# A mixer-and-FFN layer on one core: staging of the first projection, order of units, and where softmax is normalized

## The chip, the cores and the metric

The kernel runs on one core of a Trainium2 chip. The metric is the device time of one execution in microseconds (us); lower is better. The engines are TensorE (PE: matmuls, and PEld for its weight loads), VectorE (DVE), ScalarE (ACT), GpSimd (POOL) and SyncE (SP). SP and POOL only issue transfers here; the sixteen DMA engines carry them. Each engine takes its instructions in the order in which the program lists them.

## What is computed

One layer of a streaming encoder over 1088 tokens: 1024 of a new stream (the prompt) and 64 of a running one (the sample), of width 1024.

```python
h    = rmsnorm(x, g_mix)
cb, cc, ch, q, k, v, ga, gb = split(h @ w_in)      # 512 x6, 1024 x2 columns
ya   = (cb * causal_conv3(cc * ch)) @ w_conv_out
s    = q @ k.T / 8 + rel_bias[clip(i - j)]          # band: own chunk of 64 and 8 before; 8 heads of 64
o    = softmax(s) @ v                               # sample: keys and values of the caches too
yb   = o @ w_attn_out
x    = x + (sigmoid(ga) * ya + sigmoid(gb) * yb) @ w_out
x    = x + (silu(n @ w1) * (n @ w3)) @ w2           # n = rmsnorm(x, g_ffn)
y    = rmsnorm(x, g_final)
```

Besides y, the kernel stores the rolled caches: the newest 512 key and value rows of the prompt and of the sample (for the sample 448 old rows and 64 new ones), and two rows of the convolution's input for each.

## The kernel before

Every product is done in fp32 by parts: `split` (L117, L118) makes a high part by a cast on ACT and a low part by a subtraction on DVE, and three matmuls (high x high, high x low, low x high; L292 to L294 in `product`, or L456 to L458) add up one product. A transfer from or to DRAM is issued by SP unless said otherwise.

The stages, in order of time:

1. *First projection* (0 to 97 us). The nine token tiles go through in the order 8, 0, 1, 4, 2, 5, 3, 6, 7 (`ORDER`). `load_x` fetches a tile into one of three slots of 1024 columns in the scratch tile `scr`; `normed` squares it on ACT into the slot SQ (L382), makes the factor, and scales the tile on DVE with `gm` (L384), which L367 writes once; `turned1` transposes it on TensorE (L398), and casts and sums of it follow. `v_tile` multiplies it with the weights of v, and `put_v` splits the result into a single slot VST and stores it to `v_d`. The values of the last 512 prompt tokens and of the sample are also copied into SQ (L462) and stored to the outputs by POOL. Meanwhile POOL copies bias tables 0 and 1 from DRAM to DRAM (tile 3 of the order) and 448 rows of each cache to the outputs (tile 5).
2. *Twelve units* (to 365 us). Each is one pair of 128-column blocks of q, k, cc, ch, cb or gb, by Strassen's scheme (L234); ACT's L222 and L525 and DVE's adds bring its sums out of PSUM. In this stage `cache_tile` splits the old rows of the caches for k_d and v_d, and x_d and u_d (convolution's result) are written.
3. *Gates and attention* (to 614 us). Twelve gate blocks `g` (each four pieces of 24 matmuls, 128x272) are computed from weights whose load and split run ahead (`prep`, tiles rawp, whp, wlp), and stored to ga_d and gb_d. After a piece, `between` advances attention by PER steps, as long as it has any. A step does the scores of one tile of 128 queries of a head (L836, L837), its `softmax` (maximum L794, exponential with row sum L804, reciprocal L805, scaling L806), the transposes of the tile two steps back (L866, split into pt), and the values of a pair three steps back (L878, L891) with `combine` (L812 to L814), which writes o_d. At the fourth tile (t = 3) of a head, `head_load` issues the loads of k, q, v and bias of the next head, and the copy of a later bias table is asked for; the memsets L784 and L785 then write parts of the bias. Before the last LAST gates all remaining attention steps are drained.
4. *Merge* (645 to 744 us). Where the last LAST gates begin, u is loaded and o in four parts: `ol` (one buffer) is loaded, then split into `ob`. Then for eight column blocks ya = u @ w_conv_out, yb = ob @ w_attn_out, with sigmoid of ga and gb loaded again, give `mg`.
5. *Output projection, FFN up, FFN down* (744 to 1559 us), which the change does not touch.

The instructions of an engine are put in their order when the program is built, by a scheduler that looks at data and buffers; the lines give the dependences, not the order in full.

Of the kernel before, what the change touches and what calls it, by code (L numbers as in the profile page):

```python
# [8 lines left out]
F32 = mybir.dt.float32  # L9
# [27 lines left out]
PER = 2.25  # L37
LAST = 2
# [26 lines left out]
def encoder_kernel(ctx: ExitStack, tc: tile.TileContext, ins, outs):  # L65
# [19 lines left out]
    nc.gpsimd.dma_start(cols[:, :20], ins["cols"])  # L85
# [13 lines left out]
    o_d = dr.tile([ATT, T], F32, name="o_d")  # L99

# [7 lines left out]
    tables = {}  # L108

    def bias_table(h):  # L110

        tables[h] = dr.tile([P * 384], F32, tag="bias_d", name=f"bias_d{h}", bufs=2)
        nc.gpsimd.dma_start(tables[h].rearrange("(p n) -> p n", n=384), bias_rows(h, 384, 384))
# [147 lines left out]

    def prep(upto):
        while prep.n < min(upto, len(plan)):
            ld, kt, at = plan[prep.n]
            if "raw" not in ld:
                raw = rpool.tile([P, kt, ld["w"]], F32, tag="raw", name=f"rawp{prep.n}")
                nc.sync.dma_start(raw, ld["src"].rearrange("(k p) n -> p k n", p=P))
                ld["raw"] = raw
            w = []
            for k in range(0, kt, 4):  # L270
                hi, lo = (ws.tile([P, 4, P], F32R, tag=t, name=f"{t}p{prep.n}_{k}") for t in ("wh", "wl"))
                split(hi, lo, ld["raw"][:, k : k + 4, at : at + P])
                w.append((hi, lo))
            plan[prep.n] = w
            prep.n += 1
# [40 lines left out]
    X, GM, SUMS, KEPT, VST, SQ, FEW = (0, 1024, 2048), 3072, 4096, (5120, 6144), 7168, 8192, 9216  # L316
# [12 lines left out]
    def put_v(st, src, n, row):  # L329
        st = st.bitcast(F32R).rearrange("p (h l d) -> p h l d", h=NH, l=2)  # L330
        s = src.rearrange("p (h d) -> p h d", h=NH)
        split(st[:n, :, 0, :], st[:n, :, 1, :], s[:n])
        nc.sync.dma_start(
            v_d[:, row : row + n, :].rearrange("h t e -> t h e"),
            st[:n].rearrange("p h l d -> p h (l d)").bitcast(F32),
        )
# [3 lines left out]
    def load_x(i):  # L340
        t0, n = TT[i]
        a = X[len(xts) % 3]
        xts[i] = scr[:, a : a + D]
        nc.sync.dma_start(xts[i][:n], x_rows(i))
# [15 lines left out]
    load_x(ORDER[2])  # L360
# [87 lines left out]
    def v_tile(i):  # L448
# [10 lines left out]
        put_v(scr[:, VST : VST + D], pv, n, t0 if t0 < TP else TP + CACHE)  # L459
# [10 lines left out]
    for nm, u in (  # L470
        ("q", 0), ("q", 1), ("k", 0), ("k", 1), ("gb", 0), ("cc", 0), ("ch", 0), ("cb", 0), ("gb", 1), ("cc", 1),
        ("ch", 1), ("cb", 1),
    ):
        base = {"q": C_Q, "k": C_K, "cc": C_CC, "ch": C_CH, "cb": C_CB, "gb": C_GB}[nm]
        units.append((nm, u, w_in[:, base + 2 * u * P : base + 2 * (u + 1) * P]))
# [10 lines left out]
    for n, i in enumerate(ORDER):  # L486
        if n + 1 < len(ORDER):
            turned1(ORDER[n + 1])
        if n + 3 < len(ORDER):
            load_x(ORDER[n + 3])  # L490
        if n + 2 < len(ORDER):
            normed(ORDER[n + 2])
        if n == 3:
            bias_table(0)
            bias_table(1)
        if n == 4:
            u0 = unit_of(0)
        if n == 5:
            u1 = unit_of(1)

            for nm in ("k", "v"):
                nc.gpsimd.dma_start(
                    outs[f"cache_{nm}_sample"][: CACHE - TS], ins[f"cache_{nm}"].rearrange("t h d -> t (h d)")[TS:]
                )
# [163 lines left out]
    def cache_tile(i):  # L668
        ct = cts[i]
        put_v(slot(CC, 2 * ATT), ct[:, ATT:], P, TP + i * P)  # L670
# [13 lines left out]
    class PlainNext:  # L684
        def prep(self, step):
            if step == 2:
                prep(1)
            elif step == 5:
                prep(2)
# [16 lines left out]
    for n in range(len(units)):  # L706
        if n == 0:
            r, si = r0, 2
        else:
# [3 lines left out]
            else:  # L713
                new = [(PlainNext(), {})]
            if n == 1:
                ahead += new
                r, si = r1, 2
            else:
                r, si = run1(n, unit, new), 0
# [41 lines left out]
    heads = {}  # L761

    def head_load(h):
# [3 lines left out]
        for l in range(2):  # L767
# [14 lines left out]
            b[:, 384:], tables[h][127 : 127 + P * 383].rearrange("(p n) -> p n", n=383)[:, :256]  # L782
# [5 lines left out]
    def softmax(s, ps, bias, n, nm):  # L788
# [3 lines left out]
        sm = at_pool.tile([P, 1], F32, tag="sm", name=f"sm{nm}", bufs=3)[:rows]  # L792
        rc = at_pool.tile([P, 1], F32, tag="rc", name=f"rc{nm}", bufs=3)[:rows]
# [11 lines left out]
        vec.reciprocal(rc, sm)  # L805
        vec.tensor_scalar_mul(s, s, rc)  # L806
# [16 lines left out]
    def scores(h, t):  # L823
# [10 lines left out]
        for i in range(parts):  # L834
# [3 lines left out]
        b0 = 640 - n if t < 8 else 0  # L838
        softmax(
            s[:r, :n], ps[:r, :, :w] if parts == 2 else ps[:r, 0, :w], bias[:r, b0 : b0 + n], n, f"{h}_{t}"  # L840
        )
        return s
# [54 lines left out]
    def attention():  # L897
        order = [(h, t) for h in range(NH) for t in range(9)]
        done = []
        for i in range(len(order) + 3):  # L900
            if i < len(order):
                h, t = order[i]
                if t == 3 and h + 1 < NH:
                    head_load(h + 1)
                    if h + 3 < NH:
                        bias_table(h + 3)
# [21 lines left out]
    bias_table(2)  # L928
    for i in range(2):
        gate_w[i] = next_w()  # L930
        gate(i, (0, 1))
    for i in range(2):
        for c in (2, 3):
            gate(i, (c,))
            if i:
                between()
    for i in range(2, len(GATES)):
        gate_w[i] = next_w()
        if i == len(GATES) - LAST:
# [6 lines left out]
            mp = pg_stack.enter_context(tc.tile_pool(name="mgp", bufs=5, reuse_waits="tile"))  # L946
            for k in range(4):
                nc.sync.dma_start(u.t[:, :, k].bitcast(F32), u_d[k])
                t = mp.tile([P, T], F32, tag="ol", name=f"ol{k}", bufs=1)
                nc.sync.dma_start(t, o_d[k * P : (k + 1) * P])  # L950
                split(ob.t[:, 0, k], ob.t[:, 1, k], t)
# [578 lines left out]
```

## Time and profile before

| | |
|---|---|
| runs | 1568.69 us median of 3 (1564.74 to 1569.67) |
| profiled execution | 1561.12 us, its span 1559.3 us |
| PE busy in the span | 1481.3 us (95%) |
| DVE, ACT, POOL busy | 1008.3, 681.7, 70.5 us |
| granted clock of TensorE, mean | 0.988 |
| largest transfers by bytes | q1 (issued by SP) 203.74 MB, q0 (by POOL) 53.10 MB |

How to read the rows: a row of the timeline holds start, duration, engine, line, operation, output<-input, shapes, and in brackets the idle time of the engine just before with what ended it. In the table of waits there stand total, count and longest. Group rows hold count, busy total, mean ns, then idle time before. A window row holds the busy time of each engine with counts, the granted clock, the share of the DMA engines and GB/s. Transfers have KB each and the us from issue to landing.

### The profile page before, as it was taken

What the parts mean: (1) busy time and instruction counts of PE and PEld (TensorE: products, weight loads), DVE (VectorE), ACT (ScalarE), POOL (GpSimd) and SP (SyncE); (2) the same over time, 40 slices, a digit from 0 to 9 for tenths busy, and PEclk for the clock granted to TensorE, in tenths of its full rate; (3) what the DMA queues carried; (4) which work ended last, traced back from release to release, by engine and by line L of the source; (5) the groups of instructions that cost most, each with busy time, mean ns of one, the idle gap of its engine ahead of it and who ended that gap; (6) DMA issues with size and microseconds to landing.
All of it is one profiled execution on the core that took longest, in us unless ns stands there. A gap on an engine that the chain in (4) does not pass through costs nothing.

```text
span 1559.3 us, 26380 instructions
## 1 busy us (share of the span) xinstructions
PE 1481.3 (95%) x10178; PEld 1387.8 (89%) x10178; DVE 1008.3 (65%) x1989; ACT 681.7 (44%) x1382; POOL 70.5 (5%) x133
## 2 busy tenths in 40 slices
PE   5699999997999999999998999999999999899998
PEld 4589999996989889999787999999999999688886
DVE  4684556552678776566179766666666767846677
ACT  4564433331656665554056444444444444513123
POOL 1100000000000000000000000011011110000000
PEclk9899999998999999999999999999999999999999
DMA  8558654338755543853442333444444347776675
GB/s 265 167 152 218 174 155 66 126 55 242 204 159 159 154 133 110 268 165 111 140 153 95 102 124 129 144 153 144 147 153 144 134 152 261 275 233 233 218 262 204
DMA packets 178269, 260.62 MB, mean 167 GB/s; under 512 B 21328, under 2 KB 118240, under 8 KB 177984
## 3 DMA queue, kind: packets, MB, share of 16 engines
q1 hardware_dynamic: 162400, 203.74, 43.4%
q0 software_dynamic: 14592, 53.10, 9.2%
q10 hardware_dynamic: 1152, 2.10, 0.4%
q8 instruction: 80, 1.31, 0.3%
q14 instruction: 45, 0.37, 0.1%
HBM read 170.41 MB, written 91.89 MB: 168 GB/s over the span
## 4 chain that ended last, share of the span: by engine, by line
issue 73%; PE 17%; POOL 3%; DMA 3%; DVE 2%; ACT 1%; SPq 0%; POOLq 0%; ACTq 0%
PE A L1447 7%; PE D L1447 3%; POOL h_d L1168 2%; PE B L1447 2%; PE Ab L234 1%; DMA w2r<-in_w_ff 1%; PE Aa L234 1%; PE ys L1305 1%; DMA wv<-in_w_in 1%; PE Db L234 1%; PE Da L234 1%; DMA h_d<-hq 0%; PE Bb L234 0%; POOL x_d L1057 0%; POOL x_d L1070 0%
## 5 line engine op out<-in xcount | busy, mean ns | idle before, releaser
L1447 PE MATMUL A<-ring,ht 128*128 128x512 f32 x528 | 125.0, 390 | 4.2 <-ACT acc L1457 2.5
L1447 PEld LDWEIGHTS A<-ring,ht 128*128 128x128 f32 x528 | 98.7, 188 | 26.3 <-ACT acc L1457 3.8
L292 PE MATMUL g<-xn,whp 128*128 128x272 f32 x384 | 113.5, 296 | 1.1 <-ACT scr L525 1.0
L294 PE MATMUL g<-xn,wlp 128*128 128x272 f32 x384 | 112.4, 293 | 0.0
L293 PE MATMUL g<-xn,whp 128*128 128x272 f32 x384 | 112.3, 293 | 0.0
L117 ACT CAST ring<-w2r 128x512 fp32r<-128x512 f32 (+1 forms) x78 | 43.4, 588 | 105.1 <-PE A L1447 51.2
L117 ACT CAST hq<-sa 128x512 fp32r<-128x512 f32 x77 | 47.7, 619 | 85.1 <-DVE sa L1180 56.0
L292 PEld LDWEIGHTS g<-xn,whp 128*128 128x128 f32 x384 | 73.0, 190 | 2.0 <-ACT scr L525 1.2
L118 DVE TENSOR_TENSOR hq<-sa,hq 128x512 fp32r<-128x512 f32 x77 | 53.1, 689 | 33.0 <-ACT hq L117 32.9
L293 PEld LDWEIGHTS g<-xn,whp 128*128 128x128 f32 x384 | 73.1, 190 | 0.7
L294 PEld LDWEIGHTS g<-xn,wlp 128*128 128x128 f32 x384 | 72.9, 190 | 0.1
L118 DVE TENSOR_TENSOR wla<-rawa,wha 128x512 fp32r<-128x512 f32 x56 | 38.4, 687 | 42.3 <-ACT wha L117 42.3
L1447 PE MATMUL D<-ring,ht 128*128 128x512 f32 x264 | 62.9, 390 | 2.0 <-ACT acc L1457 2.0
L234 PE MATMUL Aa<-tt,wha 128*128 128x272 f32 x352 | 60.3, 293 | 3.5 <-ACT tt L117 3.5
L1447 PEld LDWEIGHTS D<-ring,ht 128*128 128x128 f32 x264 | 49.5, 188 | 12.6 <-ACT acc L1457 2.4
L234 PE MATMUL Ab<-tt,whb 128*128 128x272 f32 x352 | 58.9, 288 | 1.6 <-ACT whb L117 1.6
L1168 POOL DMA_DIRECT2D h_d<-hq x77 | 40.9, 532 | 421.2 <-DVE hq L118 244.0
L804 ACT ACTIVATE p<-p,mx 128x640 f32<-128x640 f32 (+5 forms) x72 | 50.9, 707 | 20.2 <-DVE mx L794 19.2
L234 PE MATMUL Ab<-mg,whb 128*128 128x272 f32 x352 | 58.4, 288 | 0.0
L234 PE MATMUL Aa<-mg,wha 128*128 128x272 f32 x352 | 58.3, 288 | 0.0
L117 ACT CAST wha<-rawa 128x512 fp32r<-128x512 f32 x56 | 34.8, 622 | 53.6 <-PE Ab L234 36.6
L118 DVE TENSOR_TENSOR ring<-w2r,ring 128x512 fp32r<-128x512 f32 (+1 forms) x78 | 48.9, 646 | 14.3 <-ACT ring L117 14.1
(510 smaller groups left out, 4346.0 us busy)
## 6 DMA issues: line engine op xcount, KB each, us to landing
h_d<-hq POOLq DMA_DIRECT2D x77, 512.0 KB, 3.5
ht<-h_d SPq DMA_DIRECT2D x154, 256.0 KB, 3.5
rawa<-in_w_ff SPq DMA_DIRECT2D x11, 1024.0 KB, 5.6
rawb<-in_w_ff SPq DMA_DIRECT2D x11, 1024.0 KB, 5.3
w2r<-in_w_ff SPq DMA_DIRECT2D x11, 1024.0 KB, 5.9
qd<-q_d SPq DMA_DIRECT2D x32, 272.0 KB, 4.6
v_d<-scr SPq DMA_DIRECT2D x12, 512.0 KB, 3.4
rawp<-in_w_in SPq DMA_DIRECT2D x6, 1024.0 KB, 12.0
```

The lines of the kernel that those rows point to most:

```text
L117: act.copy(hi, src)
L118: vec.tensor_tensor(lo, src, hi.bitcast(F32), op=ALU.subtract)
L234: mm(t[:, j, :HN], w[:, k, :], x[p][:, l, k, j * HN : (j + 1) * HN], start=p in (1, 2, 7) and k == 0 and n == 0, stop=k == 3 and n == 2, s ...
L292: mm(out, a, p, start=k == 0, stop=False)
L293: mm(out, a, q, start=False, stop=False)
L294: mm(out, b, p, start=False, stop=k == kt - 1)
L804: act.activation(s, s, AF.Exp, bias=mx, scale=-1.0, accum_out=sm)
L1168: nc.gpsimd.dma_start(h_d[p, c - 1], hq.rearrange("p i l t -> p (i l t)").bitcast(F32))
L1305: mm(ys[:, d, a : a + n], hs[:, r], w, start=first and i == at[d][0], stop=final and i == at[d][-1])
L1447: mm(t, ht[k][:, j, x], w[:, l], start=p in (1, 2, 7) and k == 0 and n == 0, stop=k == len(ks) - 1 and n == 2, skip_group_check=p in (6, 5 ...
```

## The change

It does the following, all in one file:

- x is staged in two slots, not three, and the load of a tile is asked for one tile later; v is staged in two slots, not one, and the stores to v_d go by POOL.
- The 448 old rows of both caches are stored by POOL from the tiles loaded in stage 2, not copied from DRAM to DRAM in stage 1. The bias tables of all heads are written at once in the sixth unit, by SP, through a slot of `scr`.
- The two gb units move to the end of the twelve; the first gate weight is loaded from the start of the last unit, and three weights are split during it instead of two.
- Four gates do their first two pieces ahead of attention, not two; PER goes from 2.25 to 2.1 and LAST from 2 to 1.
- `softmax` no longer scales its tile. The row sums of a head's nine tiles are kept side by side, inverted at once and stored to rc_d by POOL; in the merge's preparation the reciprocals are loaded again, spread over 64 rows a head, and multiply the part of o before its split.
- The loads of the constants `cols` go by SP, and the merge pool has four buffers in place of five.

```diff
--- before.py
+++ after.py
@@ -34,8 +34,8 @@
 C_CB, C_CC, C_CH, C_Q, C_K, C_V, C_GA, C_GB = 0, 512, 1024, 1536, 2048, 2560, 3072, 4096
-PER = 2.25
-LAST = 2
+PER = 2.1
+LAST = 1
@@ -82,7 +82,7 @@
     cols = const.tile([P, 22], F32, name="cols")
-    nc.gpsimd.dma_start(cols[:, :20], ins["cols"])
+    nc.sync.dma_start(cols[:, :20], ins["cols"])
@@ -97,6 +97,7 @@
     o_d = dr.tile([ATT, T], F32, name="o_d")
+    rc_d = dr.tile([NH, T], F32, name="rc_d")
@@ -105,12 +106,15 @@
-    tables = {}
-    def bias_table(h):
-        tables[h] = dr.tile([P * 384], F32, tag="bias_d", name=f"bias_d{h}", bufs=2)
-        nc.gpsimd.dma_start(tables[h].rearrange("(p n) -> p n", n=384), bias_rows(h, 384, 384))
+    bias_d = dr.tile([NH, P * 384], F32, name="bias_d")
+    def bias_tables(t):
+        nc.sync.dma_start(t, ins["bias_ext"][:, 384:768])
+        nc.sync.dma_start(
+            bias_d.rearrange("h (p n) -> h p n", n=384),
+            bass.AP(tensor=t.tensor, offset=t.offset, ap=[t.ap[0], [0, P], t.ap[1]]),
+        )
@@ -259,13 +263,17 @@
+    def plain_load(i):
+        ld, kt, at = plan[i]
+        if "raw" not in ld:
+            raw = rpool.tile([P, kt, ld["w"]], F32, tag="raw", name=f"rawp{i}")
+            nc.sync.dma_start(raw, ld["src"].rearrange("(k p) n -> p k n", p=P))
+            ld["raw"] = raw
...
         while prep.n < min(upto, len(plan)):
+            plain_load(prep.n)
             ld, kt, at = plan[prep.n]
-            if "raw" not in ld:
-                raw = rpool.tile([P, kt, ld["w"]], F32, tag="raw", name=f"rawp{prep.n}")
-                nc.sync.dma_start(raw, ld["src"].rearrange("(k p) n -> p k n", p=P))
-                ld["raw"] = raw
@@ -313,7 +321,7 @@
     scr = t1_pool.tile([P, 9264], F32, name="scr")
-    X, GM, SUMS, KEPT, VST, SQ, FEW = (0, 1024, 2048), 3072, 4096, (5120, 6144), 7168, 8192, 9216
+    X, GM, SUMS, KEPT, VST, SQ, FEW = (0, 1024), 2048, 3072, (4096, 5120), (6144, 7168), 8192, 9216
@@ -330,7 +338,7 @@
         split(st[:n, :, 0, :], st[:n, :, 1, :], s[:n])
-        nc.sync.dma_start(
+        nc.gpsimd.dma_start(
@@ -339,7 +347,7 @@
         t0, n = TT[i]
-        a = X[len(xts) % 3]
+        a = X[len(xts) % 2]
@@ -357,7 +365,6 @@
     load_wv(6)
-    load_x(ORDER[2])
@@ -456,7 +463,7 @@
             mm(pv[:n], b, wv[k][0], start=False, stop=k == KD - 1)
-        put_v(scr[:, VST : VST + D], pv, n, t0 if t0 < TP else TP + CACHE)
+        put_v(slot(VST, D), pv, n, t0 if t0 < TP else TP + CACHE)
@@ -468,8 +475,8 @@
     for nm, u in (
-        ("q", 0), ("q", 1), ("k", 0), ("k", 1), ("gb", 0), ("cc", 0), ("ch", 0), ("cb", 0), ("gb", 1), ("cc", 1),
-        ("ch", 1), ("cb", 1),
+        ("q", 0), ("q", 1), ("k", 0), ("k", 1), ("cc", 0), ("ch", 0), ("cb", 0), ("cc", 1), ("ch", 1), ("cb", 1),
+        ("gb", 0), ("gb", 1),
@@ -486,22 +493,13 @@
             turned1(ORDER[n + 1])
-        if n + 3 < len(ORDER):
-            load_x(ORDER[n + 3])
         if n + 2 < len(ORDER):
+            load_x(ORDER[n + 2])
             normed(ORDER[n + 2])
-        if n == 3:
-            bias_table(0)
-            bias_table(1)
...
             u1 = unit_of(1)
-            for nm in ("k", "v"):
-                nc.gpsimd.dma_start(
-                    outs[f"cache_{nm}_sample"][: CACHE - TS], ins[f"cache_{nm}"].rearrange("t h d -> t (h d)")[TS:]
-                )
@@ -667,6 +665,10 @@
         ct = cts[i]
+        a = 0 if i else TS
+        row = i * P + a - TS
+        for nm, o in (("k", 0), ("v", ATT)):
+            nc.gpsimd.dma_start(outs[f"cache_{nm}_sample"][row : row + P - a], ct[a:, o : o + ATT])
@@ -683,10 +685,8 @@
         def prep(self, step):
-            if step == 2:
-                prep(1)
-            elif step == 5:
-                prep(2)
+            if step in (1, 3, 5):
+                prep((step + 1) // 2)
@@ -704,6 +704,8 @@
     for n in range(len(units)):
+        if n == 5:
+            bias_tables(slot(STAGE, 384)[:NH])
@@ -712,6 +714,7 @@
                 new = [(PlainNext(), {})]
+                plain_load(0)
@@ -758,7 +761,7 @@
-    heads = {}
+    heads, sums = {}, {}
@@ -779,18 +782,16 @@
         nc.sync.dma_start(
-            b[:, 384:], tables[h][127 : 127 + P * 383].rearrange("(p n) -> p n", n=383)[:, :256]
+            b[:, 384:], bias_d[h, 127 : 127 + P * 383].rearrange("(p n) -> p n", n=383)[:, :256]
...
-    def softmax(s, ps, bias, n, nm):
+    def softmax(s, ps, bias, sm, nm):
...
         mx = at_pool.tile([P, 1], F32, tag="mx", name=f"mx{nm}", bufs=3)[:rows]
-        sm = at_pool.tile([P, 1], F32, tag="sm", name=f"sm{nm}", bufs=3)[:rows]
-        rc = at_pool.tile([P, 1], F32, tag="rc", name=f"rc{nm}", bufs=3)[:rows]
@@ -802,8 +803,6 @@
         act.activation(s, s, AF.Exp, bias=mx, scale=-1.0, accum_out=sm)
-        vec.reciprocal(rc, sm)
-        vec.tensor_scalar_mul(s, s, rc)
@@ -836,9 +835,24 @@
         b0 = 640 - n if t < 8 else 0
+        if t == 0:
+            sums[h] = at_pool.tile([P, 9], F32, tag="sm", name=f"sm{h}")
+        sm = sums[h]
         softmax(
-            s[:r, :n], ps[:r, :, :w] if parts == 2 else ps[:r, 0, :w], bias[:r, b0 : b0 + n], n, f"{h}_{t}"
+            s[:r, :n], ps[:r, :, :w] if parts == 2 else ps[:r, 0, :w], bias[:r, b0 : b0 + n], sm[:r, t : t + 1],
+            f"{h}_{t}",
         )
+        if t == 8:
+            vec.reciprocal(sm[:, :8], sm[:, :8])
+            vec.reciprocal(sm[:TS, 8:], sm[:TS, 8:])
+            for e in range(2):
+                nc.gpsimd.dma_start(
+                    rc_d[h, e * HT : e * HT + 512].rearrange("(t p) -> p t", p=P), sm[:, 4 * e : 4 * e + 4]
+                )
+                nc.gpsimd.dma_start(
+                    rc_d[h, e * HT + 512 : e * HT + HT].rearrange("(p t) -> p t", t=1), sm[32 * e : 32 * e + 32, 8:]
+                )
@@ -902,8 +916,6 @@
                     head_load(h + 1)
-                    if h + 3 < NH:
-                        bias_table(h + 3)
@@ -925,16 +937,14 @@
     nc.sync.dma_start(xn.t[0, 1].rearrange("p l k t -> p (l k) t").bitcast(F32), x21_d)
-    bias_table(2)
-    for i in range(2):
+    for i in range(4):
...
         gate(i, (0, 1))
-    for i in range(2):
+    for i in range(4):
...
             gate(i, (c,))
-            if i:
-                between()
-    for i in range(2, len(GATES)):
+            between()
+    for i in range(4, len(GATES)):
@@ -943,11 +953,18 @@
             ob = Acts(uo.tile([P, 2, 4, T], F32R, name="ob"))
-            mp = pg_stack.enter_context(tc.tile_pool(name="mgp", bufs=5, reuse_waits="tile"))
+            mp = pg_stack.enter_context(tc.tile_pool(name="mgp", bufs=4, reuse_waits="tile"))
...
                 nc.sync.dma_start(t, o_d[k * P : (k + 1) * P])
+                r = mp.tile([P, T], F32, tag="rc", name=f"rc{k}", bufs=1)
+                for j in range(2):
+                    src = rc_d[2 * k + j]
+                    nc.sync.dma_start(
+                        r[j * HD : (j + 1) * HD], bass.AP(tensor=src.tensor, offset=src.offset, ap=[[0, HD], [1, T]])
+                    )
+                vec.tensor_tensor(t, t, r, op=ALU.mult)
...
             gate(i, (c,))
```

## Prediction

> **What bounds the kernel now.** I read the page first, for the shares of the engines.
>
> ```profile
> span 1559.3 us, 26380 instructions
> PE 1481.3 (95%) x10178; PEld 1387.8 (89%) x10178; DVE 1008.3 (65%) x1989; ACT 681.7 (44%) x1382; POOL 70.5 (5%) x133
> ```
>
> TensorE (PE) bounds it: 1559.3 − 1481.3 = 78.0 us are left in which it does nothing, and nothing in the change takes matmuls away. So the change is worth what it does to these holes, to the clock after them, and what new holes it makes. Next I read TensorE's waits, in three stretches: the first projection (0–100 us), the border between the Strassen units and the gates (340–400), and attention up to the merge (388–650). Columns are: waiting line, releaser, total us, times, longest.
>
> ```profile
> PE xt L398 <- DVE scr L384: 17.9, 3, 10.3
> PE xt L398 <- DVE scr L153: 6.2, 1, 6.2
> PE gm_rows L366 <- DMA cols<-in_cols: 5.8, 1, 5.8
> ...
> PE s L836 <- DVE mx L794: 4.0, 1, 4.0
> PE Dcb L234 <- ACT scr L222: 3.2, 1, 3.2
> PE s L836 <- DMA qd<-q_d: 2.9, 1, 2.9
> PE s L837 <- DMA qd<-q_d: 2.3, 1, 2.3
> ...
> PE t L866 <- DVE pt L118: 10.1, 7, 2.6
> PE yb L292 <- ACT ob L117: 0.4, 1, 0.4
> ```
>
> The holes are 29.9 us in the first stretch, 12.4 at the border, 10.1 in attention, and 0.4 between attention and the merge; the rest lies in the output projection and the FFN, which the change leaves alone. Last I read the stretches with their granted clock (busy times of PE, PEld, DVE, ACT, POOL with counts, then the clock, DMA share, GB/s).
>
> ```profile
> 40.00:50.00 10.00, 2.80 (x12) 2.46 (x13) 5.71 (x17) 6.05 (x13) 0.00 (x0) 0.70 0.19 54
> 68.00:80.00 12.00, 4.84 (x22) 3.49 (x21) 4.97 (x10) 3.98 (x9) 0.57 (x1) 0.72 0.49 150
> ...
> 350.00:365.00 15.00, 11.63 (x79) 11.20 (x77) 5.79 (x12) 3.92 (x7) 0.00 (x0) 0.89 0.74 150
> 365.00:400.00 35.00, 24.89 (x174) 24.02 (x175) 5.65 (x17) 6.74 (x16) 0.00 (x0) 0.85 0.93 276
> 614.00:650.00 36.00, 35.59 (x283) 35.37 (x283) 10.42 (x17) 13.90 (x27) 0.00 (x0) 1.00 0.87 292
> ```
>
> The holes cost twice, since the clock stands at 0.70 to 0.89 around them. The last row gives the price of a matmul of 272 columns at full speed: 35.59 / 283 = 0.126 us; 24 of them, one piece of a gate, are 3.02 us.
>
> **The change, part 1: staging of v and x (gain 16 us, 9 to 19).** The ScalarE (ACT) and PE rows of the first stretch, and its transfers:
>
> ```profile
> 14.99 0.62 ACT L117 CAST whv<-wv 128x512 fp32r<-128x512 f32 x1 [1.01 <-DMA wv<-in_w_in]
> 15.63 1.02 ACT L367 ACTIVATE scr<-gm_rows 128x1024 f32<-128x1024 f32 x1
> 40.31 0.58 ACT L117 CAST scr<-pvv 128x512 fp32r<-128x512 f32 x1 [5.22 <-DMA v_d<-scr]
> 72.22 0.58 ACT L117 CAST scr<-pvv 128x512 fp32r<-128x512 f32 x1 [5.05 <-DMA v_d<-scr]
> 77.64 1.06 ACT L382 ACTIVATE scr<-scr 128x1024 f32<-128x1024 f32 x1 [3.50 <-DMA out_cache_v_prompt<-scr]
> ...
> 18.02 1.11 PE L398 MATMUL xt<-ident,scr 64*128 64x64 f32 x8 [10.30 <-DVE scr L384]
> 23.91 0.39 PE L458 MATMUL pvv<-whv,xs 128*64 128x512 f32 x1
> 26.68 0.39 PE L458 MATMUL pvv<-whv,xs 128*64 128x512 f32 x1
> 28.29 1.03 PE L398 MATMUL xt<-ident,scr 128*128 128x128 f32 x8
> 47.20 3.82 PE L398 MATMUL xt<-ident,scr 128*128 128x128 f32 x16 [7.21 <-DVE scr L384]
> ...
> scr<-in_x_prompt SPq DMA_DIRECT2D x8, 512.0 KB, 3.8
> v_d<-scr SPq DMA_DIRECT2D x7, 512.0 KB, 4.0
> x_d<-xn POOLq DMA_DIRECT2D x4, 512.0 KB, 4.9
> ```
>
> The one v slot holds ACT twice for 5 us until its store has landed. Behind it in ACT's order stand the squares (L382) of the next tiles, whose norm (L384) TensorE's transposes await: the holes of 7.21 and 6.18 us. With two slots a cast waits for the store of the tile before last. A tile is 24 matmuls of 512 columns, 0.231 us each ((26.68 − 23.91) / 12), and 8 transposes of 1.03 together: 6.6 us of TensorE. So that store has over 6 us beyond its landing of 4.0 on SP, or some 4.9 on POOL by the x_d row, a store of the same bytes and rows. Both holes go: 13.4 us. With them goes the slow clock: the 16 transposes at 47.20 take 3.82 where 8 take 1.03 at speed, 1.8 us too many, and the second hole costs about 0.9 likewise: 2.7 together.
>
> The start moves too. ACT's L367 (15.63), which all norms need, stands behind the cast that waits for wv until 14.99; in the changed program it stands ahead of that cast; the third x load, the bias tables and the two cache copies leave the time in which wv lands. The constants come first on SP's queue. I take 3.8 us of the 10.30 (none to 5).
>
> Against this: x has two slots instead of three. The load of tile n+2 waits for the transposes of n. From there it takes 3.8 for landing, 1.06 + 0.19 for the square, 1 for the factor, 1.3 for the norm, about 7.5, against two tiles of TensorE, 13; it fits by 5 us unless the square queues behind something. The slot of the squares is also that of the 32-bit v (3.50 at 77.64), with its store now behind v's on POOL's queue: 1 to 2 us a time. I take off 4: 13.4 + 2.7 + 3.8 − 4 = 16. Low end: no gain at the start and 7 lost in slots, 9; high end: 1 lost, 19.
>
> The cache stores and v's stores are issued by POOL, 5% busy; SP's queue, past which they move, is freed of a wait, so loads behind them come earlier. The tables' 1.5 MB now go over SP in unit 5; a unit takes (364 − 97) / 12 = 22 us and loads 1 MB of weights besides: 0.
>
> **Part 2: order of units, gates' first pieces (gain 11 us, 6 to 13).**
>
> ```profile
> 355.87 0.62 ACT L117 CAST whp<-rawp 128x512 fp32r<-128x512 f32 x1 [6.54 <-DMA rawp<-in_w_in]
> 374.36 0.65 ACT L117 CAST scr<-scr 128x544 fp32r<-128x544 f32 x1 [8.58 <-DMA u_d<-scr]
> ```
>
> ACT waits for the gates' first weights, and the copy L222 behind it lets TensorE wait 3.23 us. The changed program loads that weight from the start of the last unit, and splits in three steps: gone. With gb last, u's store is two units earlier: the 8.58 us before the cast, which let k and q of head 0 come late, go too. And four gates' first halves, 8 pieces = 24.2 us instead of 12.1, lie ahead of the first score: cover for the loads of head 0 and for the bias wait of 4.0. So 3.2 + 4.0 + 2.9 + 2.3 + 1.0 (a gate behind L525) = 13.4, of which I leave 2.4: the first gate still waits for the last unit's end, and a load may come late. Low end: the gates' cover doesn't reach the 4.0 and half the loads, 6.
>
> **Part 3: reciprocals off VectorE (gain 3 us, 8 to a loss of 3).** From the groups on VectorE (DVE) in 380–620:
>
> ```profile
> L806 DVE TENSOR_SCALAR p<-p,rc 128x640 f32<-128x640 f32 (+5 forms) x72 | 33.0, 467 | 0.9
> L805 DVE RECIPROCAL rc<-sm 128x1 f32<-128x1 f32 (+1 forms) x72 | 10.6, 154 | 10.6 <-ACT p L804 10.5
> ...
> L784 DVE MEMSET bias<- 64x64 f32 x8 | 0.9, 112 | 25.3 <-DMA bias<-in_bias_ext 25.2
> ```
>
> Away go 33.0 + 10.6 = 43.6 us of DVE, and its wait of 10.6; 16 reciprocals of about 0.15 come, 2.4. TensorE shows only 10.1 us of holes here, one a head, and they fall where DVE waits in the memset L784 for the next head's bias (25.3 us). That wait stays: the same loads stand behind the same stores in SP's order. A freer DVE has less queued when the bias lands; so a third of 10.1. The four stores of 4-byte sums a head, on POOL, are read 20 us and more later, save the last head's: hidden.
>
> **Part 4: from attention to the merge (loss 23 us, 18 to 27).** `ol` is one buffer: load, cast, subtract, next load.
>
> ```profile
> 631.89 1.10 ACT L117 CAST ob<-ol 128x1088 fp32r<-128x1088 f32 x1 [5.49 <-DMA ol<-o_d]
> 646.46 1.10 ACT L117 CAST ob<-ol 128x1088 fp32r<-128x1088 f32 x1 [0.47 <-DMA ol<-o_d]
> ...
> 612.92 0.92 PE L878 MATMUL pv<-pts,vsd 128*128 128x128 f32 x5
> 640.00 1.29 DVE L118 TENSOR_TENSOR ob<-ol,ob 128x1088 fp32r<-128x1088 f32 x1 [5.68 <-ACT ob L117]
> ...
> ol<-o_d SPq DMA_DIRECT2D x4, 544.0 KB, 4.5
> ```
>
> A turn is 4.5 + 1.10 + 1.29 + 0.2 = 7.1 us, and the fourth cast (646.46) came 32.7 us after attention's last matmuls (613.8). Over that time TensorE had two gates, 244 matmuls or 30.7 us to the point where it needs the fourth part: 0.4 us of hole. The change lays on both sides of this. A multiply of the same shape as the subtract (1.29) goes into each turn: 8.4 with its hand-over. And LAST = 1 leaves one gate behind attention: 84 matmuls by the program's order, then ya and yb until the fourth part's turn, 142 in all, 17.9 us. Nothing else may run ahead of them on TensorE. The first multiply stands behind the last gate weights' subtracts on DVE, 12 us after attention's end, its cast is done at 14.4; three turns more, 14.4 + 3 × 8.4 = 39.5. So TensorE idles 39.5 − 17.9 = 21.6 where it idled 0.4. Low end: the first multiply comes when ol and rc land, 4 us earlier: 18. High end: rc's broadcast load delays each turn by 1: 25 and the clock, 27. After the fourth wait TensorE starts slowly as at 47.20, which cost 1.8: loss 21.2 + 1.8 = 23.
>
> The Trainium skill, "TensorE: Matmul & The Clock Gate", section "HAM oscillation", says that waits above about 3.4 us let the clock fall to half until some 3.4 us of work have passed. The trace agrees: 0.70 in 40–50. By it the waits between the parts cost nothing more (their work is shorter than the wait), and the last one 1.7 us in place of my 1.8.
>
> ga and gb have four buffers instead of five: TensorE has no wait on them in the merge of before, and a piece's chain is short of four pieces: 0.
>
> **The sum** against the profiled execution, 1561.12 us (span 1559.3 and 1.8 around it): −16 − 11 − 3 + 23 = −7, 1554.1. That execution lies 7.6 below the median of the runs shown, 1568.69; on the median's scale the forecast is 1561.7, −0.4%. Its own range is ±8.
>
> **Rivals.** *A, the merge's stall doesn't bite.* If ob's parts come before TensorE needs them (loads landing in 2 us, or the merge starting with ya alone), part 4 is 0: −30, 1538.7; with half of it, 1550. For it: ya needs no ob. Against: yb's first matmul stands behind 12 of ya in the program.
> *B, the bias wait reaches TensorE (slower).* In attention the whole wait at L784, 25.3 us instead of 10.1, shows on TensorE, because more gates lie ahead and fewer steps of cover behind each bias load: +15.2 and no gain of 3: +11.2, 1579.9. It decides from some 1.5 us more a head. For it: the wait is there once a head. Against: the same loads, and a freer DVE.
> *C, the x slots eat the start.* If squares queue behind the casts, loads of x land as slowly as others under load, and the first 97 us stay: part 1 falls to 4 and the border to 8: +8, 1576.7; half of that, 1569, no change.
>
> **How the numbers follow.** Forecast 0.50, A 0.14, B 0.16, C 0.20. A measurement here tells no change to within 0.3%, 4.7 us. Below 1564.0 lie 0.7 of the forecast, A, and little of C: 0.50. Above 1573.4 lie B, half of C and a little of the forecast: 0.27. Between: 0.23. The range reaches to A's half and into B: 1548 to 1578.
>
> **What would show it.** Right: no ACT wait on v_d in the first 100 us, the first unit (L234) starting near 81 instead of 97; TensorE gaps under 3 us in all around the first scores; memset waits as before; about four waits of yb on ACT's ob, 20 us in all, after attention. Wrong: waits of L398 on the norm or of the norm on x loads; yb not waiting; L866 waiting over 15 us.

## The result and the profile after

The changed kernel takes 1618.80 us (median of 4 runs, 1616.67 to 1621.55) against 1569.18 us before (1564.74 to 1575.44): 1.0314 times as long, 95% interval 1.0275 to 1.0353. It is slower by 49.6 us where 7 us of gain were forecast. Its profiled execution took 1621.55 us, so on the side of the traces the difference is 1619.6 − 1559.3 = 60.3 us. Some 11 us of this belong to the two executions and not to the change: the one of before (1561.12) lies 8.1 us under its median, the one after 2.8 over. Lengths of stages below are of one execution each.

The head of the page of the changed kernel:

```profile
span 1619.6 us, 26436 instructions
PE 1505.9 (93%) x10178; PEld 1408.2 (87%) x10178; DVE 984.9 (61%) x1865; ACT 682.8 (42%) x1382; POOL 101.2 (6%) x175
```

Its waits of TensorE in attention and merge, 362 to 800 us (waiting line, releaser, total us, times, longest):

```profile
PE s L835 <- DVE mx L795: 31.5, 7, 7.2
PE yb L300 <- ACT ob L121: 19.2, 4, 5.5
PE t L880 <- DVE pt L122: 6.6, 8, 4.4
```

TensorE issues the same 10178 matmuls and is busy 24.6 us longer: that is slow clock (granted 0.969 in the mean, before 0.988). The rest of the 60.3 is 35.7 us of holes, in which TensorE does nothing. These three rows hold 57.3 us where the same waits held 14.5 before (4.0, 0.4 and 10.1, shown in the prediction); elsewhere there is less. Where they lie is read from the starts of four groups of instructions, which cut both traces into stages. In the timeline of before, then of after:

```profile
97.09 0.66 PE L234 MATMUL Aq<-xn,whq 128*128 128x272 f32 x4
365.83 0.40 PE L292 MATMUL g<-xn,whp 128*128 128x272 f32 x1 [0.97 <-ACT scr L525]
734.77 0.40 PE L1021 MATMUL wo<-woh,ms 128*128 128x512 f32 x1
```

```profile
82.77 0.66 PE L238 MATMUL Aq<-xn,whq 128*128 128x272 f32 x4
362.37 0.39 PE L300 MATMUL g<-xn,whp 128*128 128x272 f32 x1 [0.97 <-ACT scr L523]
657.52 0.92 PE L892 MATMUL pv<-pts,vsd 128*128 128x128 f32 x5
794.29 0.40 PE L1038 MATMUL wo<-woh,ms 128*128 128x512 f32 x1
```

With attention's last matmuls at 612.92 before (shown ahead of the prediction) and their ends at 613.8 and 658.4:

| stage | before | after | difference |
|---|---|---|---|
| first projection, to Aq | 97.1 | 82.8 | −14.3 |
| twelve units, Aq to the first g | 268.7 | 279.6 | +10.9 |
| attention, first g to the end of pv | 248.0 | 296.1 | +48.1 |
| merge, end of pv to wo | 120.9 | 135.8 | +14.9 |
| the rest | 824.5 | 825.3 | +0.8 |

LAST = 1 moves gate work from the merge's stage into attention's: the traces count 190 matmuls of gates after attention's end before and 84 after, so 106 moved, 13.3 us at 0.126 us each. Without this move attention loses 48.1 − 13.3 = 34.8 us and the merge 14.9 + 13.3 = 28.2.

The waits of the changed kernel's VectorE in 375 to 660 us show two that end with a transfer: the memset of the bias, as before, and the last write into co_s, which waits for a store into o_d.

```profile
DVE bias L787 <- DMA bias<-in_bias_ext: 43.8, 7, 21.8
DVE co_s L813 <- DMA o_d<-co: 31.4, 6, 8.1
```

The first row is larger than the 25.2 us of before, but 35.6 of its 43.8 lie ahead of 410, and the first sums are stored at 418; after 410 it is 8.2 us, where before has 9.9. The second row is the new one: before has no such wait. It points at transfers that land late. The view of transfers for the ten microseconds 518 to 528, while a head's sums are stored to rc_d (POOL issues the four stores from 515.9 to 520.1):

```profile
DMA  8999980000000297949999008994099499890646
...
DMA packets 223, 0.33 MB, mean 33 GB/s; under 512 B 53, under 2 KB 117, under 8 KB 223
...
q1 hardware_dynamic: 191, 0.32, 80.1%
q0 software_dynamic: 32, 0.00, 1.9%
...
qd<-q_d SPq DMA_DIRECT2D x4, 272.0 KB, 14.4
```

In before, over attention, 380 to 620 us:

```profile
qd<-q_d SPq DMA_DIRECT2D x28, 272.0 KB, 4.3
...
o_d<-co SPq DMA_DIRECT2D x32, 64.0 KB, 2.6
```

The DMA engines are busy at seven tenths or more in about half of the 40 slices (first row) and move 33 GB/s; over attention before they moved 153. Loads of qd land after 14.4 us, before after 4.3. By the trace the stores' own packets (q0, POOL's queue) take 1.9% of the engines' time here, those of SP's queue (q1) 80.1%: it is the others' packets that take long.

In the stretches with these waits TensorE's granted clock is lower. Windows of the changed kernel (start:end, length, busy times of PE, PEld, DVE, ACT, POOL, granted clock, DMA share, GB/s):

```profile
500.00:550.00 50.00, 41.98 (x282) 39.49 (x281) 26.98 (x68) 26.22 (x58) 2.59 (x4) 0.87 0.70 131
550.00:600.00 50.00, 42.08 (x289) 38.82 (x287) 26.54 (x66) 24.97 (x61) 5.18 (x8) 0.93 0.71 125
...
680.00:706.00 26.00, 11.11 (x44) 9.95 (x44) 10.42 (x13) 7.94 (x14) 0.00 (x0) 0.63 0.84 268
```

### The profile page after: what moved, and what is told of

Same layout as the page of the kernel before. It is cut to its first block, busy times and chain, and to the rows that moved or that the text cites. A ratio compares the mean times of both kernels' runs of the same rounds, so it can differ in the third digit from the quotient of the medians.

```text
span 1619.6 us, 26436 instructions
## 1 busy us (share of the span) xinstructions
PE 1505.9 (93%) x10178; PEld 1408.2 (87%) x10178; DVE 984.9 (61%) x1865; ACT 682.8 (42%) x1382; POOL 101.2 (6%) x175
## 4 chain that ended last, share of the span: by engine, by line
PE 65%; DMA 13%; issue 11%; DVE 5%; ACT 2%; POOL 1%; SPq 1%; another core or an unknown queue 0%; ACTq 0%; POOLq 0%; DVEq 0%
PE A L1464 6%; PE Ab L238 6%; PE Aa L238 6%; DMA o_d<-co 4%; PE D L1464 3%; PE Db L238 3%; PE Da L238 3%; PE B L1464 2%; PE g L302 2%; PE g L300 2%; PE g L301 2%; PE Bb L238 1%; PE Agb L238 1%; PE t L880 1%; PE Acc L238 1%
## 5 line engine op out<-in xcount | busy, mean ns | idle before, releaser
L300 PE MATMUL g<-xn,whp 128*128 128x272 f32 x384 | 117.6, 306 | 1.0 <-ACT scr L523 1.0
L301 PE MATMUL g<-xn,whp 128*128 128x272 f32 x384 | 114.4, 298 | 0.0
L300 PEld LDWEIGHTS g<-xn,whp 128*128 128x128 f32 x384 | 76.5, 199 | 1.9 <-ACT scr L523 1.2
L302 PEld LDWEIGHTS g<-xn,wlp 128*128 128x128 f32 x384 | 76.2, 199 | 0.8
L301 PEld LDWEIGHTS g<-xn,whp 128*128 128x128 f32 x384 | 76.4, 199 | 0.1
L795 DVE CUSTOM_DVE_ANT_0 p<-s,bias 128x640 f32<-128x640 f32 (+5 forms) x72 | 47.4, 660 | 34.4 <-PE s L836 30.2
L835 PE MATMUL s<-kd,qd 128*128 128x320 f32 (+2 forms) x96 | 33.3, 353 | 33.3 <-DVE mx L795 31.5
```

The lines of the kernel that those rows point to most:

```text
L300: mm(out, a, p, start=k == 0, stop=False)
L301: mm(out, a, q, start=False, stop=False)
L302: mm(out, b, p, start=False, stop=k == kt - 1)
L795: vec.tensor_tensor_reduce(out=s if len(ps.shape) == 2 else s.rearrange("p (a b) -> p a b", a=2), in0=ps, in1=bias if len(ps.shape) == 2 e ...
L835: mm(ps[:r, i, :w], q[0][:, qs], k[:, ksl], start=True, stop=False)
```

## The experiments

The time of each run stands beside that of the kernel before measured together with it, 1570.1 to 1571.6 us in the median. Stage lengths are read as above. "Pacing" in the expectations means LAST, PER and the gates put first.

### What the stores of 4-byte sums cost

*b_rc*, the kernel before with the four stores of a head added:

```diff
+        if t == 0:
+            sums[h] = at_pool.tile([P, 9], F32, tag="rc", name=f"rc{h}")
...
+        if t == 8:
+            for e in range(2):
+                nc.gpsimd.dma_start(
+                    rc_d[h, e * HT : e * HT + 512].rearrange("(t p) -> p t", p=P), sm[:, 4 * e : 4 * e + 4]
+                )
...
```

> The kernel before, with the stores of the reciprocals alone added: the reciprocals of a head's nine tiles are kept side by side as in the changed kernel and stored to rc_d by POOL in the same four transfers of 4-byte elements per head; nothing reads rc_d. Theory (element stores): the stores hold the DMA engines for some 8 to 10 us a head, loads and stores of SP behind them land late, and TensorE waits and then runs at a slow clock: 25 to 40 us more than before, 1594 to 1610, with TensorE's holes in attention at 25 us or more in place of 10. Rival (pacing: the loss in attention comes from LAST, PER and the gates put first): within 3 us of before, 1566 to 1572.

Measured: 1636.22 us, 1.0425 times before (1.0286 to 1.0565), 65.5 us more, from two executions that lie far apart (1627.32, which is the profiled one, and 1645.11); the expectation named the mechanism and fell short of the size. Attention takes 307.4 us instead of 248.0. Its waits of TensorE:

```profile
PE t L878 <- DVE pt L119: 37.4, 6, 9.7
PE s L836 <- DVE mx L794: 19.8, 9, 3.9
```

So 57 us of holes where before had 14, from stores whose data nobody reads. Nothing of LAST, PER or the gates was touched: the loss needs no pacing.

*b_rc16* differs from b_rc in one size, the bytes that lie together in rc_d:

```diff
-                    rc_d[h, e * HT : e * HT + 512].rearrange("(t p) -> p t", p=P), sm[:, 4 * e : 4 * e + 4]
+                    rc_d[h, e * HT : e * HT + 512].rearrange("(p t) -> p t", t=4), sm[:, 4 * e : 4 * e + 4]
```

> The kernel before with the stores of the reciprocals added as in the run b_rc, but the four values that a partition holds for a half go to neighbouring places, so that one element is 16 B: 128 + 32 elements a half instead of 512 + 32, the same number of transfers, bytes and waits. Nothing reads rc_d. Theory (the price is per element): b_rc lost 65 us, so 320 / 1088 of that, some 19 us: 1584 to 1596. Rival (the price is per transfer, or lies in POOL's queue): 55 to 65 us as with b_rc, 1625 or more.

Measured: 1588.51 us, 17.0 us more than its 1571.55 before; forecast was some 19. 65.5 us over 8 x 1088 elements is 7.5 ns an element, 17.0 over 8 x 320 is 6.6; by the two intervals it may be 5 to 10 and 4 to 8. Bytes, transfers and waits are equal, so the price goes by the number of elements, or by their size, which changes with it. The Trainium skill, "DMA: Bandwidth & Descriptors", section "Rules for kernel authors", says that a last dimension that is not contiguous becomes one descriptor per element. The times agree with it, but the traces don't count descriptors: their packets on POOL's queue are 32 a store in b_rc, b_rc16 and a_rows alike. The landing of these stores in the three runs, in attention, follows the number of elements.

```profile
rc_d<-rc POOLq DMA_DIRECT2D x12, 2.0 KB, 10.8
...
o_d<-co SPq DMA_DIRECT2D x23, 64.0 KB, 9.8
```

```profile
rc_d<-rc POOLq DMA_DIRECT2D x13, 2.0 KB, 4.8
...
o_d<-co SPq DMA_DIRECT2D x24, 64.0 KB, 6.1
```

```profile
rc_d<-rr POOLq DMA_DIRECT2D x14, 2.0 KB, 3.5
...
o_d<-co SPq DMA_DIRECT2D x32, 64.0 KB, 1.9
```

The 2 KB themselves land after 10.8, 4.8 and 3.5 us, and the stores of o_d, which only share the DMA engines with them, after 9.8, 6.1 and 1.9 (before: 2.6). VectorE's wait of co_s for them is 21.0 us in b_rc, 2.7 in b_rc16, and absent in a_rows, while the wait for the bias stays in a_rows (47.4 us).

*a_rows*, the changed kernel with the same values stored as rows:

```diff
+            nc.tensor.transpose(tp[:8, 640:768], sm[:, :8], ident)
+            nc.tensor.transpose(tp[:1, 768 : 768 + TS], sm[:TS, 8:], ident[:TS, :TS])
+            rr = at_pool.tile([8, P + TS], F32, tag="rr", name=f"rr{h}")
+            vec.tensor_copy(rr[:, :P], tp[:8, 640:768])
+            vec.tensor_copy(rr[:1, P:], tp[:1, 768 : 768 + TS])
...
+                    rc_d[h, e * HT : e * HT + 512].rearrange("(t p) -> t p", p=P), rr[4 * e : 4 * e + 4, :P]
```

> The changed kernel, but the reciprocals of a head are transposed on TensorE (two small transposes a head), copied out by VectorE, and stored in rows of 512 B and 128 B. Theory (element stores): 25 to 40 us less than the changed kernel, 1579 to 1594, TensorE's wait on L795 in attention down from 31.5 us to under 10, the stall of yb on ob still about 20. Rival (pacing): no gain, 1616 to 1622.

Measured: 1587.54 us, 1.0115 times before (1.0060 to 1.0171): 31.3 us less than the changed kernel. Attention falls from 296.1 to 261.0 us, as long as before with the 106 gate matmuls more (248.0 + 13.3 = 261.3). The same stores that cost 65.5 us in b_rc cost about half of it here; why their price depends so much on the program around them was not tried. The merge's stall stays, as the waits of 365 to 770 us show:

```profile
PE yb L300 <- ACT ob L121: 18.0, 4, 5.4
PE s L835 <- DVE mx L795: 9.4, 6, 4.4
```

### What the multiply in the merge costs, and what VectorE gained

*a_old*: the changed kernel without the sums, rc_d and the multiply; each tile is scaled in softmax as before.

```diff
+        vec.reciprocal(rc, sm)
+        vec.tensor_scalar_mul(s, s, rc)
...
-                vec.tensor_tensor(t, t, r, op=ALU.mult)
```

> The changed kernel with softmax as before: reciprocal and scaling per tile, no rc_d, no multiply of ol in the merge's preparation; all other edits stay. Theory (element stores): like the kernel with row stores or better, since a turn of ol is 1.3 us shorter four times (5 us less stall of yb): 1573 to 1590. Rival (a freer VectorE matters): slower than the kernel with row stores by over 5 us. Rival (pacing): 1612 to 1620.

Measured: 1564.08 us, 0.9973 times before (0.9948 to 0.9998), 23.5 us less than a_rows and under the range expected. The merge falls from 135.1 in a_rows to 118.1, its wait of yb on ob from 18.0 to 2.0 us:

```profile
PE s L839 <- DVE mx L797: 7.3, 4, 4.4
PE yb L300 <- ACT ob L121: 2.0, 2, 1.3
```

And attention, with 43.6 us of VectorE's work back in it, is not longer but shorter: 255.6 in place of 261.0. Of these 5.4 us, 3.7 are busy time of TensorE that a_rows has more, most of it the transposes of the sums (3.9). Its waits on VectorE are no shorter in a_rows, 11.0 us (s 9.4 and t 1.6) against 8.8 (7.3 and 1.5). So no gain shows from taking this work away; a run with the relief and without any store was not made.

*a_last2*: the changed kernel with two gates left for the merge.

```diff
-PER = 2.1
-LAST = 1
+PER = 2.35
+LAST = 2
```

> The changed kernel with LAST = 2 (and PER = 2.35, so that 32 calls still advance all 75 steps). Theory (short cover): the four waits of yb on ob, 19.2 us, all but vanish, and with them some 3 us of slow clock; 1594 to 1602. The holes in attention stay. Rival (the wait of ob only moves, or attention is squeezed in the shorter time): less than 8 us gained.

Measured: 1610.60 us, 8.2 us less, where 17 to 25 were expected. The waits of 362 to 800 us tell why:

```profile
PE yb L300 <- ACT ob L121: 7.8, 2, 4.5
PE t L880 <- DMA vsd<-v_d: 7.0, 1, 7.0
...
PE ya L300 <- DMA u<-u_d: 4.5, 1, 4.5
PE g L300 <- ACT gst L759: 3.5, 1, 3.5
```

11.4 us of yb's waits go, so the second gate is cover indeed, and L835's (not shown here) fall from 31.5 to 19.3; but 15 us of other waits come, for v, for u and in the gates. Whether LAST or PER brings these was not tried.

### Where the first projection's gain comes from, and where it goes

The trace of before has more at the start than the program's order suggests. POOL issues two table copies and a cache copy while wv lands, and the six other tables at 60.6 us:

```profile
2.32 1.10 POOL L113 DMA_DIRECT2D bias_d<-in_bias_ext  x2
3.41 0.50 POOL L502 DMA_DIRECT2D out_cache_k_sample<-in_cache_k  x1
...
60.61 3.23 POOL L113 DMA_DIRECT2D bias_d<-in_bias_ext  x6
```

*b_stage*, the kernel before with the new slots alone (diff of the core; the loads of x move as in the change, cache rows stay on SP):

```diff
-    X, GM, SUMS, KEPT, VST, SQ, FEW = (0, 1024, 2048), 3072, 4096, (5120, 6144), 7168, 8192, 9216
+    X, GM, SUMS, KEPT, VST, SQ, FEW = (0, 1024), 2048, 3072, (4096, 5120), (6144, 7168), 8192, 9216
...
-        put_v(scr[:, VST : VST + D], pv, n, t0 if t0 < TP else TP + CACHE)
+        put_v(slot(VST, D), pv, n, t0 if t0 < TP else TP + CACHE)
```

> The kernel before with the staging of x (two slots), of v (two slots, stored by POOL in the first stage) and the constants on SP, and nothing else; the bias tables and cache copies stay in the first stage. Theory (the v slot made the holes): the first unit starts at 82 to 86 us in place of 97 as in the changed kernel; 10 to 16 us less than before, 1554 to 1560. Rival (the copies of tables and caches made them): the first unit starts later than 92.

*b_nocopy*, the other half alone: slots as before, but the cache copies and tables go out of the first stage as in the change.

```diff
-            for nm in ("k", "v"):
-                nc.gpsimd.dma_start(
-                    outs[f"cache_{nm}_sample"][: CACHE - TS], ins[f"cache_{nm}"].rearrange("t h d -> t (h d)")[TS:]
-                )
...
+        if n == 5:
+            bias_tables(slot(STAGE, 384)[:NH])
```

> The kernel before with the cache copies and bias tables of the first stage taken out and done as in the changed kernel (cache rows stored by POOL from the loaded tiles, tables by SP in the sixth unit); staging of x and v as before. Theory (their bytes stand in the way of wv and x at the start and change what the scheduler puts first): the first unit starts at 82 to 88 us. Rival (it needs both, no copies and two v slots): later than 91. Time not under 1563, since the tables cost something in the units.

*b_stage2* has both edits:

> The run b_nocopy with the staging of the changed kernel (two slots of x, two of v stored by POOL in the first stage, constants on SP). Both theories: the first unit starts at 82 to 85 us as in the changed kernel. If b_nocopy shows the same, the slots are worth nothing; if b_nocopy starts at 91 or later, only the two together work.

| | before | b_stage | b_nocopy | b_stage2 | changed kernel |
|---|---|---|---|---|---|
| first stage, us | 97.1 | 96.1 | 80.3 | 82.8 | 82.8 |
| units, us | 268.7 | 280.1 | 297.3 | 290.7 | 279.6 |
| sum | 365.8 | 376.2 | 377.6 | 373.5 | 362.4 |
| median over before | | 1.0002 (0.9989 to 1.0016) | 1.0031 (1.0009 to 1.0054) | 1.0013 (0.9988 to 1.0039) | 1.0314 |

The start of the first unit in b_stage and b_nocopy:

```profile
96.09 0.66 PE L234 MATMUL Aq<-xn,whq 128*128 128x272 f32 x4
```

```profile
80.35 0.66 PE L236 MATMUL Aq<-xn,whq 128*128 128x272 f32 x4
```

The slots alone are worth 1 us, the copies and tables moved out 17, both together 14; b_stage fits its rival, and b_nocopy its theory, a little under the range. In b_nocopy, with the one slot, ACT's wait for the store of v falls from 10.3 to 3.6 us, and the first tile's transposes start at 13.28 us instead of 18.02. The timeline of b_stage, two rows of ACT and one of TensorE, shows the step that failed: the cast of v no longer waits for its store, but for TensorE, and the squares still stand behind it in ACT's order.

```profile
39.46 0.59 ACT L117 CAST scr<-pvv 128x512 fp32r<-128x512 f32 x1 [3.02 <-PE pvv L457]
39.94 1.06 ACT L381 ACTIVATE scr<-scr 128x1024 f32<-128x1024 f32 x1
...
44.76 3.68 PE L397 MATMUL xt<-ident,scr 128*128 128x128 f32 x16 [5.33 <-DVE scr L383]
```

And in b_stage's first stage the squares wait for the loads of x, which have two slots instead of three:

```profile
ACT scr L381 <- DMA scr<-in_x_prompt: 7.8, 4, 3.3
```

This is the condition of rival C. So the 1.0 us can be a gain by the slot of v and a loss by those of x; the two were not run apart.

How far one execution can be trusted here, two groups of runs show. b_rc and b_rc16 leave the program ahead of attention as in before: their first stage takes 98.2 and 99.1 us, their units 271.7 and 273.1. a_rows, a_old and a_last2 leave it as in the changed kernel: 82.7 to 83.8, and 278.3 to 281.9. So the first stage gained some 15 us and the units lost some 9, and b_stage's units, in its slowest execution of ten, say little. By the medians b_nocopy and b_stage2 are no faster than before, so what their first stage wins is given back, by the stages mainly in the units. In b_nocopy TensorE's waits in the units begin with late weights:

```profile
PE Ak L236 <- ACT whk L119: 8.1, 1, 8.1
PE Acb L236 <- ACT whcb L119: 5.0, 1, 5.0
PE Acb L236 <- ACT scr L224: 4.1, 1, 4.1
```

What the changed kernel has beyond b_stage2 up to this point is the order of units, the earlier gate weights, and split cache rows stored by POOL: 373.5 − 362.4 = 11 us, in one execution each.

Two runs on a_old asked what costs the units time. *c_tab* writes the tables by POOL, *c_cache* stores the split cache rows by SP:

```diff
+        for h in range(NH):
+            nc.gpsimd.dma_start(bias_d[h].rearrange("(p n) -> p n", n=384), bias_rows(h, 384, 384))
```

> The run a_old with the bias tables written in the sixth unit by eight transfers of POOL from DRAM to DRAM, not by SP through a slot of scr. Theory (the one write of 1.5 MB from 8 partitions holds the DMA engines and a slot): TensorE's waits of Acc on the weights of cc, 4.1 us, and the slow clock behind them go; 4 to 8 us less than a_old, 1556 to 1561. Rival (these waits come from the order of units): within 2 us of a_old.

```diff
-        put_v(slot(CC, 2 * ATT), ct[:, ATT:], P, TP + i * P)
+        put_v(slot(CC, 2 * ATT), ct[:, ATT:], P, TP + i * P, nc.sync)
```

> The run a_old with the split cache rows stored to v_d by SP as in the kernel before, not by POOL; the output stores of the cache stay with POOL. Theory (POOL's queue makes these stores late): the waits of Aq on L533 and L226 around 100 to 113 us, some 4 to 5 us with slow clock, go: 4 to 6 us less than a_old. Rival (they come from two slots shared by loads and splits, whoever stores): within 2 us of a_old.

Measured: c_tab 1564.66 us (0.9948 of before, 0.9933 to 0.9963), c_cache 1565.54 (0.9958, 0.9940 to 0.9977), a_old 1564.08: neither is apart from a_old in the median, as the rivals said, and against before all three are a little faster, by 0.3 to 0.5%. In the traces c_cache's units take 275.4 us and c_tab's 276.2, where a_old has 280.0; the waits of Aq are gone in c_cache, and that of Acc falls from 4.1 to 0.2 in c_tab. But c_tab's first stage is 88.6 instead of 82.7. Its eight transfers depend on nothing and were put first on POOL:

```profile
L114 POOL DMA_DIRECT2D bias_d<-in_bias_ext x8: 523/523/681, 1.3 to 5.4; - x8
```

### A version faster than both

*c_best* is c_cache with the gates, PER, LAST and five merge buffers of before; *c_best2* is c_best with the tables written as before.

```diff
-PER = 2.1
-LAST = 1
+PER = 2.25
+LAST = 2
...
-    for i in range(4):
+    for i in range(2):
         gate_w[i] = next_w()
         gate(i, (0, 1))
```

> The run c_cache with the gates, PER, LAST and merge buffers of the kernel before. It keeps the first stage, the order of units and the earlier gate weights of the changed kernel. Theory (pacing brought nothing): attention and merge take 363 to 369 us together, in place of 373.8 in c_cache and 368.9 before, and the whole 1552 to 1560. Rival (the gates put first are worth their place): 1566 or more.

> The run c_best with the bias tables as in the kernel before (one transfer of POOL a head from DRAM to DRAM, two buffers), not in one write of SP in the sixth unit. Theory (that write costs the units some 4 us; two tables at the start cost the first stage less): units 272 us or less in place of 276.1, first stage 82 to 85, 1 to 4 us less than c_best. Rival (the early tables cost the first stage as much as they spare the units, as with c_tab): within 1 us of c_best.

c_best: 1561.98 us, 0.9940 of before (0.9915 to 0.9964): a small gain, but clear of its interval; by the medians it is 3.5% under the changed kernel. Of the changes that bear on the time it differs from b_stage2 (1572.09) only by the order of units and the earlier gate weights, which are worth 10.1 us here; on the kernel before they were not tried alone. Attention and merge take 248.6 + 121.5 = 370.1 us against 373.8 in c_cache, so the pacing of the change brought nothing: apart from the 13.3 us of matmuls moved, c_cache is 8 us shorter in attention and 12 longer in the merge. The time is 2 us over the expected range. c_best2: 1567.39 us, 0.9987 (0.9967 to 1.0006), a miss: the tables went to the front again, the first stage takes 87.1 us against 81.8, and the units 280.9 against 276.1. So without the write of the tables in the sixth unit the units are longer here and shorter in c_tab, by 4 to 5 us each: its share stays open.

## Why the prediction was wrong, point by point

- **Part 3 failed, and with it the sign.** The step is "The four stores of 4-byte sums a head, on POOL, are read 20 us and more later, save the last head's: hidden." It asked when their data is needed, and not what 1088 single elements a head do to the transfers of others. b_rc and b_rc16 show it: 65.5 and 17.0 us by the number of elements. In place of 3 us gained, attention lost 34.8, and stored in rows (a_rows) it lost none. Rival B had the right place and sign, TensorE waiting in attention, but another cause, the wait for the bias: this is as long in a_rows, where attention has its old length; its price of 15.2 us was also too low.
- **The relief of VectorE shows no gain.** a_old has the scaling back and a shorter attention than a_rows, and TensorE waits no longer for VectorE in it. The 3 us taken for it are not borne out, though no run has the relief alone.
- **Part 4 was right, and too small by 5 us.** Forecast loss 23, measured 28.2: four waits of yb on ob, 19.2 us, as foretold, and the clock at 0.63 in 680 to 706. VectorE's multiplies in the changed kernel show the turn of 8.4 us exactly on the mean, (698.87 − 673.62) / 3:

```profile
673.62 1.29 DVE L967 TENSOR_TENSOR ol<-ol,rc 128x1088 f32<-128x1088 f32 x1 [3.17 <-DMA rc<-rc_d]
...
698.87 1.29 DVE L967 TENSOR_TENSOR ol<-ol,rc 128x1088 f32<-128x1088 f32 x1 [5.49 <-DMA ol<-o_d]
701.32 1.29 DVE L122 TENSOR_TENSOR ob<-ol,ob 128x1088 fp32r<-128x1088 f32 x1 [1.16 <-ACT ob L121]
```

  The first came 3 us later than reckoned, 15.2 instead of 12 us after attention's end, and so the fourth part was cast 42.9 us after it (701.32 − 658.4) instead of 39.5. The other 2 us are not traced further. The prediction did not part the two causes: with LAST = 1 and without the multiply (a_old) the wait is 2.0 us and the merge loses 118.1 + 13.3 − 120.9 = 10.5, so the multiply with its loads makes some 17 of the 28. In a_old the fourth part is cast 32.4 us after attention's end, and TensorE does 32 more matmuls, 27 of them of yb, before it needs it.
- **Part 1 had the right size by luck, for a wrong reason.** The first unit starts 14.3 us earlier, forecast 16. The step "With two slots a cast waits for the store of the tile before last", by which "Both holes go", fails in b_stage, which gains 1.0 us; b_nocopy gains 16.8 with the one slot. What was listed as a side matter, the copies and tables at the start, carried all of it: taking the named releaser away left the holes, since in b_stage other waits end as late and ACT's order still puts the squares behind the cast. c_tab and c_best2, with tables at the front and no cache copies, lie between, at 88.6 and 87.1 us; by what path the copies delay the stage was not traced.
- **The other side of part 1 was left out.** The tables and cache stores moved into the units were put at 0 there; the units lost 10.9 us (some 9 by the two groups of runs) while two short holes at their end (3.2 and 1.0, of which the second stayed) were to go. 14.3 gained and 10.9 lost leave 3.4. Split cache rows stored by POOL may hold some 4 us of it: the units take 275.4 and 276.1 us in c_cache and c_best, which store them by SP, and 278.3 to 281.9 in the four runs that store them by POOL and write the tables alike; the medians of c_cache and a_old don't show it. The rest stays open.
- **Part 2 was half right.** The hole at Dcb is gone. At the first scores 1.2, 1.2 and 4.4 us are left of 9.2: the wait for the bias (4.0) did not go in spite of 24 us of cover. Of the 13.4 us listed, 5.6 came.

## What to carry to other kernels

Before you move a reduction's small results through DRAM, count the elements that do not lie side by side: 35 KB in 8704 pieces made the changed kernel 31.3 us and the kernel before 65.5 us longer, to spare 43.6 us of VectorE from which no gain shows. Transpose such a tile into rows first if it must go. A transfer nobody waits for can still delay others, so price an added store by what shares the DMA engines with it. A releaser named in a profile may be only the last of several things late: take it away alone (one run) before crediting its holes to it, and look for the same work at the place where moved bytes arrive.

## What was not expected of the hardware

A store of 2 KB in 4-byte elements took 10.8 us to land; with 16-byte elements it took 4.8 us, in rows of 512 B 3.5. In ten microseconds around such stores of the changed kernel all transfers together came to 0.33 MB, though the engines were far from idle, and it was the packets of the other queue that filled 80.1% of their time, not those of the stores (1.9%). What holds the others was not tried.
